# A two-layer decoder trunk on one core: later turns at the feed-forward ends, and attention scores over 128 rows with padded queries

## The chip, the core and the metric

The kernel runs on one core of a Trainium2 chip. The metric is the device time of one launch, in microseconds, as the median of the runs. Engines are named as the profile names them: PE (TensorE, matrix products), PEld (its weight loads), DVE (VectorE), ACT (ScalarE), POOL (GpSimd), SP (SyncE, which issues the weight DMAs).

## The reference

A sequence of 256 tokens of width 2048 goes through two layers, in fp32. Cut to what matters here:

```python
def reference(x, mem, ...):
    for i in range(2):
        if i == 1:
            sk1, sk2, sv = shared_kv(x, kv_norm, w_kv, k_norm, cos, sin)   # 12 heads, keys of 64, values of 128
        u = rms_norm(x, mix_norm[i]) @ w_in[i]
        if i == 0:
            ...                       # causal pooling in four groups
        else:
            q1 = partial_rope(rms_norm(q1, q_norm[b]), cos, sin)    # 12 heads of 64, two maps
            q2 = partial_rope(rms_norm(q2, q_norm[b]), cos, sin)
            o = differential_attention(q1, q2, sk1, sk2, sv, lam)
            token_out = rms_norm(o, subln_norm[b]) * (1.0 - lam_init)
        mem_out = memory_cross_attention(mem_q, mem, ...)           # 4 heads of 128 over 256 memory rows
        x = x + concat(token_out, mem_out) @ w_out[i]
        h = relu(rms_norm(x, ffn_norm[i]) @ w_ff1[i])
        x = x + (h * h) @ w_ff2[i]                                  # width 8192 between
    return x

def differential_attention(q1, q2, k1, k2, v, lam):
    def probs(q, k):
        s = einsum('bqhd,bkhd->bhqk', q, k) * dk ** -0.5
        return softmax(where(key_pos <= q_pos, s, -1e30))
    a = probs(q1, k1) - lam * probs(q2, k2)
    return einsum('bhqk,bkhd->bqhd', a, v)
```

## The kernel before

Activations are held transposed, as tiles of 128 channels by 256 tokens: the residual `resid` is `[128, 16, 256]`. The weights do not fit on the core and are streamed. `Feed.load` brings 128x1024 floats by a DMA from SP, and `Feed._split` turns each block of 512 columns into a rounded half (`hi_ring`, ACT, L147) and the rest (`lo_ring`, DVE, L148), in a ring of six slots, three jobs ahead. Activations are split in the same manner (`split_gain`, ACT L353 and DVE L284; `x_kv` and `x_mx` are two such splits of the residual, with two gains). A product is the sum of high by high, high by low and low by high.

PE goes through the stages in the order of the program: memory keys and values, input projection and pooling of layer 0, its memory heads, `w_out`, the feed-forward part `ffn(0)`; then for layer 1 the shared keys (three `k1` tiles) and values (`v1`), memory keys and values (`mk1`, `mv1`), three `q1` tiles with the differential heads, four memory heads, `w_out`, `ffn(1)` and the output. Steps that are not a product of the stage itself (scores, turns, normalisations) are queued by hand: `at(d, fn)` puts `fn` behind `d` ticks, and `tick()` comes once for four weight blocks. `flush()` runs all that is still queued. So the order on PE is written out; a wait of one queued step holds all PE work behind it.

**The feed-forward part.** `down_tile` (L679 to L706) multiplies one of eight column tiles of the first half of `w_ff2` and gets its bank from `bank()` (tag "st", one buffer); `evict` (L628 to L631) copies the bank to `room` on ACT, and one tick later two DVE adds (L701, L702) put it on `resid` and `done(n)` is called. The second half of the columns is computed from 2x2 block products with fewer multiplications (`slab_jobs`, `product` L711 to L717), summed in seven banks. `last` (L808 to L818) runs the last quarter: the remaining slabs, then `down_tile` for n = 0 to 7; ahead of n = 5 `finish_banks` (L755) combines the seven banks, and queues four `turn(h)` (L773 to L783), at ticks 6 to 9. Each turn is four PE transposes into one bank (`ct`, tag "t", one buffer), one DVE add of 128x512 to `resid` (L781), and `done` for two channel tiles. In layer 0 `done` is `resid_done` (L602): split `x_kv`, then `add_square`, which squares on POOL (L595, the first L589) and adds on POOL (L596) to `acc`. `columns("x")` (from L406) multiplies `acc` by a constant on PE (`tc_x`, L410) for the row norms that scale k1, v1 and q1. In layer 1 `done` is the output DMA.

**The differential heads.** `kT` holds the keys transposed: two heads of 64 lie in the 128 rows of one tile, for each of the two maps. `turn_rows` transposes a pair of heads' queries of both maps in four PE transposes and writes them to `qb` with one ACT copy of 128x512 (L509). `diff_head(h, ...)` queues `scores` (L1113 to L1141), four ticks later `turn` (`dt`, L1146), two ticks after that `pv` (`do`, L1152 to L1154), and three ticks later `back` (`o_t`, L1175). Scores are, for each map, a matmul over the 64 rows of the head, followed by a bf16 matmul of the identity by the mask:

```python
kk = kT[hh : hh + 64, 6 * m + j, :]
nc.tensor.matmul(s1[:, m, :], q[hh : hh + 64, P:T], kk, start=True, stop=False)
nc.tensor.matmul(s1[:, m, P:T], idb, mkb, start=False, stop=True)
```

`s1` is for the second 128 queries against all 256 keys (L1118, L1119), `s0` for the first 128 against 128 keys (L1122, L1123).

Of the kernel before, what the change touches and what calls it, by code (L numbers as in the profile page):

```python
# [10 lines left out]
F32 = mybir.dt.float32  # L11
# [235 lines left out]
def program(ctx, tc, plan, dry, xT, memT, par, lam, cst, wst, yT):  # L247
# [16 lines left out]
    def at(d, fn):  # L264
        pend.setdefault(now[0] + d, []).append(fn)
# [6 lines left out]
    def flush():  # L272
        while pend:
            tick()


    def vt(name):
        return tp.tile([P, T], F32, tag="v", bufs=6, name=name)

    def mmt(name):  # L280
        return pp.tile([P, 512], F32, tag="mm", bufs=3, name=name)
# [42 lines left out]
    def gcol(c):  # L324
        return param[:, c : c + 1]
# [26 lines left out]
    def split_gain(dst, src, g):  # L352
        nc.scalar.activation(dst[:, 0:T], src, AF.Copy, scale=g)  # L353
        stt(dst[:, T : 2 * T], src, g, dst[:, 0:T].bitcast(F32), ALU.mult, ALU.subtract)
# [146 lines left out]
    def turn_rows(raw, i, dst, g):  # L501

        t4 = pp.tile([P, 2, T], F32, tag="t", bufs=1, name="tr")
        for c in range(2):
            for t in range(2):
                nc.tensor.transpose(
                    t4[:, c, t * P : t * P + P], raw[:, t, (i + c) * P : (i + c) * P + P], ident
                )
        nc.scalar.activation(dst, t4, AF.Copy, scale=g)  # L509
# [75 lines left out]
    def add_square(key, src, first, act=False):  # L585

        if first:
            acc[key] = tp.tile([P, T], F32, tag="acc", bufs=1, name="acc")
            nc.gpsimd.tensor_mul(acc[key], src, src)  # L589
            return  # L590
        sq = vt("psq")
        if act:
            nc.scalar.activation(sq, src, AF.Square)
        else:
            nc.gpsimd.tensor_mul(sq, src, src)  # L595
        nc.gpsimd.tensor_add(acc[key], acc[key], sq)  # L596

    def resid_add(ps, n):
        nc.vector.tensor_add(resid[:, n, :], resid[:, n, :], ps[:, 0:T])
        nc.vector.tensor_add(resid[:, n, :], resid[:, n, :], ps[:, T : 2 * T])  # L600

    def resid_done(n, splits):  # L602
        for dst, g in splits:
            split_gain(dst[:, n, :], resid[:, n, :], gcol(g + n))
        add_square("x", resid[:, n, :], n == 0)


    def ffn(l, xs, tags, done):
# [99 lines left out]
        def bank():  # L708
            return pp.tile([P, 512], F32, tag="st", bufs=1, name="x_bank")
# [45 lines left out]
        def finish_banks():  # L755

            p1, p2, p5, p6, p3, p7, p4 = banks
            low = tp.tile([P, 2, 512], F32, tag="rows", bufs=3, name="c_a")
            upp = tp.tile([P, 2, 512], F32, tag="rows", bufs=3, name="c_b")
            c11, c12 = upp[:, 0, :], upp[:, 1, :]  # L760
            u, v = low[:, 0, :], low[:, 1, :]
            add, sub = nc.vector.tensor_add, nc.vector.tensor_sub
            nc.scalar.copy(u, p1)
            nc.scalar.copy(v, p5)
            add(c11, u, p2)
            add(u, u, p6)
            sub(c12, v, u)
            add(u, u, p7)
            add(c12, c12, p3)
            sub(v, v, u)  # L770
            sub(u, u, p4)

            def turn(h):  # L773
                c = 8 + 2 * h
                t4 = pp.tile([P, 2, T], F32, tag="t", bufs=1, name="ct")
                for e in range(2):
                    n = (2 * h + e) // 4
                    w = (2 * h + e) % 4 * P
                    for t, side in enumerate((upp, low)):
                        nc.tensor.transpose(t4[:, e, t * P : t * P + P], side[:, n, w : w + P], ident)  # L780
                nc.vector.tensor_add(resid[:, c : c + 2, :], resid[:, c : c + 2, :], t4)  # L781
                done(c)
                done(c + 1)  # L783

            for h in range(4):
                at(6 + h, lambda h=h: turn(h))

        groups = ((0,), (1, 2), (3,))
        for i in range(NK):
# [18 lines left out]
        def last(q=3):  # L808
            slabs = {0: (0, 1), 1: (2, 3), 2: (4, 5), 3: (6,), 4: (7,)}
            for n in range(8):  # L810
                for i in slabs.get(n, ()):
                    run = slab_jobs(q, i)
                    for j in range(4):
                        run(j)
                        tick()
                if n == 5:
                    finish_banks()
                down_tile(q, n, bank())  # L818

        return last  # L820

# [185 lines left out]
    out_tiles(0, cat, [lead0], [0, 1, 2], fx, last_group)  # L1007

    x_in = []
    down = ffn(0, fx, ("S1", "S0"), lambda n: resid_done(n, [(x_in[0], G_KV)]))  # L1010
    x_kv = sp.tile([P, NK, 512], F32R, tag="S2", name="x_kv")
    x_in.append(x_kv)
    down()
    flush()
    x_mx = sp.tile([P, NK, 512], F32R, tag="S0", name="x_mx")
    for n in range(NK):
        at(10 + 2 * n, lambda n=n: split_gain(x_mx[:, n, :], resid[:, n, :], gcol(G_MIX + 16 + n)))


    kv = sp.tile([P, 6144], F32, tag="big", name="big1")  # L1020
# [25 lines left out]
        return [mmt(name) for _ in range(2)]  # L1046

    c1 = []
    at(6, lambda: c1.extend(columns("x")))
    for c in range(3):  # L1050
        ps = pair_of_banks(c, "k1")
        b_tile(ps, "w_kv", 0, c, x_kv)
# [33 lines left out]
    def carve(n):  # L1086
        off[0] += n
        return att[:, off[0] - n : off[0]]
# [3 lines left out]
    ab = [carve(384) for _ in range(2)]  # L1092
    aTb = [carve(384) for _ in range(2)]
    pT1 = carve(512).rearrange("p (a t) -> p a t", a=2)
    qb = [carve(512).rearrange("p (m t) -> p m t", m=2) for _ in range(4)]
    em1 = [carve(512).rearrange("p (a t) -> p a t", a=2) for _ in range(2)]

    gsub = cp.tile([P, 1], F32, name="gsub")
    nc.vector.tensor_scalar_mul(gsub, gcol(G_SUB), 1.0 - LAM_INIT)
# [4 lines left out]

    cat1 = sp.tile([P, NK, 512], F32R, tag="S1", name="cat1")

    def diff_head(h, q1, q2, y, lag):
        hh = (h % 2) * 64
        j = h // 2
        e1, e0, a, aT = e1b[h % 2], e0b[h % 2], ab[h % 2], aTb[h % 2]  # L1110
        yh = y.rearrange("p (t j m h) -> p t j m h", t=2, j=2, m=2)[:, :, j % 2, :, h % 2]
# [1 line left out]
        def scores():  # L1113
            s1 = pp.tile([P, 2, T], F32, tag="s", bufs=2, name="s1")
            s0 = pp.tile([P, 2, P], F32, tag="s", bufs=2, name="s0")
            for m, q in enumerate((q1, q2)):
                kk = kT[hh : hh + 64, 6 * m + j, :]
                nc.tensor.matmul(s1[:, m, :], q[hh : hh + 64, P:T], kk, start=True, stop=False)  # L1118
                nc.tensor.matmul(s1[:, m, P:T], idb, mkb, start=False, stop=True)  # L1119
            for m, q in enumerate((q1, q2)):  # L1120
                kk = kT[hh : hh + 64, 6 * m + j, 0:P]
                nc.tensor.matmul(s0[:, m, :], q[hh : hh + 64, 0:P], kk, start=True, stop=False)  # L1122
                nc.tensor.matmul(s0[:, m, :], idb, mkb, start=False, stop=True)  # L1123
            mx = tp.tile([P, 4], F32, tag="m4", bufs=6, name="mx")
            z = tp.tile([P, 4], F32, tag="m4", bufs=6, name="z")
            for i, t, s, e in ((0, 1, s1, e1), (2, 0, s0, e0)):
                mi = mx[:, i : i + 2]
                nc.vector.tensor_reduce(out=mi, in_=s, axis=AX.X, op=ALU.max, negate=True)
                nc.vector.tensor_mul(mi, mi, yh[:, t, :])
                for m in range(2):  # L1130
                    nc.scalar.activation(
                        e[:, m, :], s[:, m, :], AF.Exp, bias=mx[:, i + m : i + m + 1],
                        scale=yh[:, t, m : m + 1], accum_out=z[:, i + m : i + m + 1],
                    )
            zr = tp.tile([P, 4], F32, tag="m4", bufs=6, name="zr")
            nc.vector.reciprocal(zr, z)
            zl = tp.tile([P, 2], F32, tag="m2", bufs=12, name="zl")
            nc.vector.tensor_scalar_mul(zl, zr.rearrange("p (i m) -> p i m", m=2)[:, :, 1], nlam)
            for i, e, dst in ((0, e1, a[:, P : P + T]), (1, e0, a[:, 0:P])):
                nc.vector.tensor_scalar_mul(e[:, 1, :], e[:, 1, :], zl[:, i : i + 1])  # L1140
                stt(dst, e[:, 0, :], zr[:, 2 * i : 2 * i + 1], e[:, 1, :], ALU.mult, ALU.add)  # L1141
# [42 lines left out]
    for c in range(3):  # L1184
        ps = pair_of_banks(0, "q1")
        b_tile(ps, "w_in_q", 1, c, x_mx)
        rows, v = query_rows(ps, c1, 64)
        rope(rows, qtab)
        y = query_scale(v, c1)
        for i in range(2):  # L1190
            j = 2 * c + i
            q = qb[j % 4]
            at(4 + i, lambda i=i, q=q, rows=rows: turn_rows(rows, 2 * i, q, qcol))
            for g in range(2):
                diff_head(2 * j + g, q[:, 0, :], q[:, 1, :], y, 6 + (2 if c == 2 else 3) * (2 * i + g))
    for h in range(4):
        ps = mmt("mq1")
        c_tile(ps, "w_in", 1, 12 + h, range(NK), x_mx)
        q, y = mem_query(ps[:, 0:T], mqg1, c1)
        mem_head(  # L1200
            q, y, mk1[:, h, :], lambda mb, h=h: mv1[:, mb, h * P : h * P + P],
            em1[h % 2], pT1, cat1[:, 12 + h, :], 3,
        )

    fx1 = sp.tile([P, NK, 512], F32R, tag="S0", name="fx1")
# [87 lines left out]
```

## Time and profile before

| what | value |
|---|---|
| runs | 2097.9, 2101.76, 2098.39 us |
| median | 2098.39 us |
| profiled execution | 2097.61 us, span 2095.8 us |
| PE clock granted, mean | 0.999 of full speed |
| PE, DVE, ACT, POOL busy | 99%, 83%, 64%, 4% of the span |
| HBM traffic | 185 GB/s over the span |

The span is the stretch between the first and the last instruction of the profiled execution; its own time is 1.8 us longer. A busy share is over the whole span; a stage may look quite different. In a line of grouped instructions stand line, engine and operation, the tiles by name (written <- read), shapes, count, busy time, mean duration of one in ns, and the idle time of the engine ahead of them with what ended it. Matmuls overlap on PE, so the step from one start to the next says what a matmul takes, and the mean duration is longer than that.

### The profile page before, as it was taken

The page shows a single profiled execution, that of the slowest core. Times are in us where ns is not written, and L with a number is a line of the kernel's source. Part 1 is how long each engine was busy: PE and PEld are TensorE (multiplying, and loading weights), DVE is VectorE, ACT ScalarE, POOL GpSimd, SP SyncE. Part 2 cuts the span into 40 slices and gives each one's busy share as a digit, 9 for nine tenths or more (in the row PEclk, how much of TensorE's full clock was granted, in tenths as well). Part 3 has the DMA queues.
Part 4 walks back from the last instruction along what each step waited for, and adds up shares of the span by engine and source line. Part 5 has one row for each costly group of instructions (what it writes and reads, how often), then busy time and mean ns, then how long its engine had stood idle before and what let it go on. Part 6 is the DMA issues. An engine that isn't in the chain of part 4 may idle for free.

```text
span 2095.8 us, 32323 instructions
## 1 busy us (share of the span) xinstructions
PE 2076.5 (99%) x11086; PEld 1755.1 (84%) x11086; DVE 1733.5 (83%) x3210; ACT 1344.4 (64%) x2483; POOL 85.8 (4%) x98
## 2 busy tenths in 40 slices
PE   9999999999999999999999999999999999999998
PEld 7888888888888888777888778888888888888877
DVE  8788888789888878999755687888878878988897
ACT  7765576566667656666655577557656666666664
POOL 0002300000000000014000000310000000000000
PEclk9999999999999999999999999999999999999999
DMA  8555555565555656554565433555556555565554
GB/s 308 171 186 188 181 191 182 186 208 189 192 192 192 209 181 204 177 169 159 190 227 191 141 122 101 194 187 184 188 181 206 191 192 197 185 209 189 192 186 141
DMA packets 110469, 390.75 MB, mean 186 GB/s; under 512 B 12256, under 2 KB 14944, under 8 KB 110304
## 3 DMA queue, kind: packets, MB, share of 16 engines
q1 hardware_dynamic: 110160, 388.59, 55.7%
q8 instruction: 87, 1.43, 0.3%
q14 instruction: 78, 0.64, 0.1%
q10 hardware_dynamic: 144, 0.10, 0.0%
HBM read 386.54 MB, written 2.10 MB: 185 GB/s over the span
## 4 chain that ended last, share of the span: by engine, by line
PE 52%; DVE 2%; ACT 1%; issue 0%; DMA 0%; POOL 0%; DVEq 0%; ACTq 0%
PE x_bank L364 9%; PE x_bank L689 6%; PE x_bank L365 4%; PE wo L364 3%; PE ff L364 3%; PE x_bank L690 3%; PE p L717 2%; PE p L715 2%; PE p L716 2%; PE ff L365 1%; PE wo L365 1%; PE q L388 1%; PE v L390 1%; PE v L388 1%; PE v L389 1%; PE q L390 1%
## 5 line engine op out<-in xcount | busy, mean ns | idle before, releaser
L147 ACT CAST hi_ring<-raw 128x512 fp32r<-128x512 f32 x1193 | 735.6, 620 | 541.5 <-PE x_bank L364 166.1
L148 DVE TENSOR_TENSOR lo_ring<-raw,hi_ring 128x512 fp32r<-128x512 f32 x1193 | 831.7, 704 | 232.9 <-ACT hi_ring L147 215.2
L364 PE MATMUL x_bank<-fx,hi_ring 128*128 128x512 f32 x1536 | 543.8, 397 | 0.0
L365 PE MATMUL x_bank<-fx,lo_ring 128*128 128x256 f32 x1536 | 429.8, 280 | 0.0
L689 PE MATMUL x_bank<-z,hi_ring 128*128 128x512 f32 x1008 | 359.3, 398 | 4.9 <-ACT room L630 3.7
L364 PEld LDWEIGHTS x_bank<-fx,hi_ring 128*128 128x128 f32 x1536 | 288.3, 188 | 75.5 <-ACT room L630 0.8
L365 PEld LDWEIGHTS x_bank<-fx,lo_ring 128*128 128x128 f32 x1536 | 289.6, 189 | 1.4
L690 PE MATMUL x_bank<-z,lo_ring 128*128 128x256 f32 x1008 | 282.7, 281 | 0.2 <-DVE lo_ring L148 0.2
L148 DVE TENSOR_TENSOR lo_ring<-slab,hi_ring 128x1024 fp32r<-128x1024 f32 x192 | 234.8, 1224 | 47.4 <-ACT hi_ring L147 37.6
L147 ACT CAST hi_ring<-slab 128x1024 fp32r<-128x1024 f32 x192 | 200.7, 1047 | 65.6 <-PE p L716 23.6
L689 PEld LDWEIGHTS x_bank<-z,hi_ring 128*128 128x128 f32 x1008 | 189.8, 188 | 55.1 <-ACT room L630 6.1
L690 PEld LDWEIGHTS x_bank<-z,lo_ring 128*128 128x128 f32 x1008 | 190.5, 189 | 3.6 <-DVE lo_ring L148 2.1
L364 PE MATMUL wo<-cat,hi_ring 128*128 128x512 f32 x512 | 182.2, 400 | 0.0
L364 PE MATMUL ff<-fx,hi_ring 128*128 128x512 f32 x512 | 179.9, 397 | 0.0
L365 PE MATMUL wo<-cat,lo_ring 128*128 128x256 f32 x512 | 143.6, 281 | 0.0
L365 PE MATMUL ff<-fx,lo_ring 128*128 128x256 f32 x512 | 142.9, 279 | 0.0
L364 PEld LDWEIGHTS wo<-cat,hi_ring 128*128 128x128 f32 x512 | 96.1, 188 | 23.8 <-DVE cat L284 0.2
L364 PEld LDWEIGHTS ff<-fx,hi_ring 128*128 128x128 f32 x512 | 96.1, 188 | 23.1
L715 PE MATMUL p<-hi_ring,sit 128*128 128x512 f32 x256 | 102.1, 399 | 1.8 <-ACT hi_ring L147 1.5
L717 PE MATMUL p<-lo_ring,sit 128*128 128x512 f32 x256 | 100.5, 396 | 1.1 <-DVE lo_ring L148 1.0
L716 PE MATMUL p<-hi_ring,sit 128*128 128x512 f32 x256 | 100.5, 393 | 0.0
L365 PEld LDWEIGHTS wo<-cat,lo_ring 128*128 128x128 f32 x512 | 96.7, 189 | 0.3
(290 smaller groups left out, 3335.9 us busy)
## 6 DMA issues: line engine op xcount, KB each, us to landing
raw<-in_w SPq DMA_DIRECT2D x595, 512.0 KB, 3.5
slab<-in_w SPq DMA_DIRECT2D x128, 512.0 KB, 3.6
resid<-in_x SPq DMA_DIRECT2D x8, 256.0 KB, 5.4
memraw<-in_mem SPq DMA_DIRECT2D x4, 512.0 KB, 3.6
out_y<-resid SPq DMA_DIRECT2D x16, 128.0 KB, 1.8
memraw<-in_mem SPq DMA_DIRECT2D x7, 256.0 KB, 6.3
raw<-in_w SPq DMA_DIRECT2D x3, 256.0 KB, 3.8
memraw<-in_mem SPq DMA_DIRECT2D x2, 128.0 KB, 4.3
```

What stands on the lines that cost most here:

```text
L147: self.nc.scalar.copy(hi, src)
L148: self.nc.vector.tensor_sub(lo, src, hi.bitcast(F32))
L364: nc.tensor.matmul(ps, hi, xs[:, k, :], start=first and i == 0, stop=False)
L365: nc.tensor.matmul(ps[:, T : 2 * T], lo, xs[:, k, 0:T], start=False, stop=last and i == len(ks) - 1)
L388: nc.tensor.matmul(ps[t], xl, hi, start=k == 0, stop=False)
L389: nc.tensor.matmul(ps[t], xh, hi, start=False, stop=False)
L390: nc.tensor.matmul(ps[t], xh, lo, start=False, stop=k == NK - 1)
L689: nc.tensor.matmul(ps, hi, z[:, i, :], start=a, stop=False)
L690: nc.tensor.matmul(ps[:, T : 2 * T], lo, z[:, i, 0:T], start=False, stop=b)
L715: nc.tensor.matmul(ps, a[1], hi, start=first, stop=False)
L716: nc.tensor.matmul(ps, a[0], hi, start=False, stop=False)
L717: nc.tensor.matmul(ps, a[0], lo, start=False, stop=last)
```

## The change

It has two parts, added together.

**Ends of the feed-forward parts.** The four turns are queued two ticks later (8 to 11). The column tiles n = 6 and 7 of the last quarter get banks of the tag "mm" (three buffers) in place of the one "st" bank. In layer 0 `resid_done` no longer squares; the squares are queued behind `down()`, two for each tick from 2 to 9, on ACT, with their sums on DVE (`later_square`). The `flush()` behind `down()` goes, so turns that are still queued come among the first k1 blocks. The splits of `x_mx` start at tick 14 in place of 10, and `columns("x")` comes at tick 12 in place of 6.

**Scores over 128 rows.** The queries of a pair of heads are written into two tiles, one for each head, whose other 64 rows are zero. The zeros are set once by six DVE memsets for three pairs of tiles, and `turn_queries` writes the 64 rows of each head by an ACT copy of its own. The scores' matmuls then take all 128 rows of `kT` and of the padded tile. `em1`, the exponentials of the memory heads, has one buffer in place of two, which makes room for the tiles.

```diff
@@ -595,14 +595,25 @@
+    def later_square(n):
+
+        if n == 0:
+            acc["x"] = tp.tile([P, T], F32, tag="acc", bufs=1, name="acc")
+            nc.scalar.activation(acc["x"], resid[:, 0, :], AF.Square)
+            return
+        sq = vt("later")
+        nc.scalar.activation(sq, resid[:, n, :], AF.Square)
+        nc.vector.tensor_add(acc["x"], acc["x"], sq)
...
-    def resid_done(n, splits):
+    def resid_done(n, splits, square=True):
         for dst, g in splits:
             split_gain(dst[:, n, :], resid[:, n, :], gcol(g + n))
-        add_square("x", resid[:, n, :], n == 0)
+        if square:
+            add_square("x", resid[:, n, :], n == 0)
@@ -783,7 +794,7 @@
             for h in range(4):
-                at(6 + h, lambda h=h: turn(h))
+                at(8 + h, lambda h=h: turn(h))
@@ -815,7 +826,7 @@
                 if n == 5:
                     finish_banks()
-                down_tile(q, n, bank())
+                down_tile(q, n, bank() if n < 6 else mmt("ff2"))
@@ -1007,14 +1018,15 @@
-    down = ffn(0, fx, ("S1", "S0"), lambda n: resid_done(n, [(x_in[0], G_KV)]))
+    down = ffn(0, fx, ("S1", "S0"), lambda n: resid_done(n, [(x_in[0], G_KV)], False))
     x_kv = sp.tile([P, NK, 512], F32R, tag="S2", name="x_kv")
     x_in.append(x_kv)
     down()
-    flush()
+    for n in range(NK):
+        at(2 + n // 2, lambda n=n: later_square(n))
     x_mx = sp.tile([P, NK, 512], F32R, tag="S0", name="x_mx")
     for n in range(NK):
-        at(10 + 2 * n, lambda n=n: split_gain(x_mx[:, n, :], resid[:, n, :], gcol(G_MIX + 16 + n)))
+        at(14 + 2 * n, lambda n=n: split_gain(x_mx[:, n, :], resid[:, n, :], gcol(G_MIX + 16 + n)))
@@ -1046,7 +1058,7 @@
-    at(6, lambda: c1.extend(columns("x")))
+    at(12, lambda: c1.extend(columns("x")))
@@ -1092,8 +1104,23 @@
-    qb = [carve(512).rearrange("p (m t) -> p m t", m=2) for _ in range(4)]
-    em1 = [carve(512).rearrange("p (a t) -> p a t", a=2) for _ in range(2)]
+    qb = [[carve(512).rearrange("p (m t) -> p m t", m=2) for _ in range(2)] for _ in range(3)]
+    em1 = carve(512).rearrange("p (a t) -> p a t", a=2)
+    for pair in qb:
+        nc.vector.memset(pair[0][64:128], 0.0)
+        nc.vector.memset(pair[1][0:64], 0.0)
+
+    def turn_queries(rows, i, pair):
+        t4 = pp.tile([P, 2, T], F32, tag="t", bufs=1, name="tq")
+        for c in range(2):
+            for t in range(2):
+                nc.tensor.transpose(
+                    t4[:, c, t * P : t * P + P], rows[:, t, (i + c) * P : (i + c) * P + P], ident
+                )
+        for g, r in enumerate((slice(0, 64), slice(64, 128))):
+            nc.scalar.activation(pair[g][r], t4[r], AF.Copy, scale=qcol[r])
@@ -1113,13 +1139,13 @@
-            for m, q in enumerate((q1, q2)):
-                kk = kT[hh : hh + 64, 6 * m + j, :]
-                nc.tensor.matmul(s1[:, m, :], q[hh : hh + 64, P:T], kk, start=True, stop=False)
+            for m in range(2):
+                kk = kT[:, 6 * m + j, :]
+                nc.tensor.matmul(s1[:, m, :], q[:, m, P:T], kk, start=True, stop=False)
                 nc.tensor.matmul(s1[:, m, P:T], idb, mkb, start=False, stop=True)
...
@@ -1189,17 +1215,17 @@
-            q = qb[j % 4]
-            at(4 + i, lambda i=i, q=q, rows=rows: turn_rows(rows, 2 * i, q, qcol))
+            q = qb[j % 3]
+            at(4 + i, lambda i=i, q=q, rows=rows: turn_queries(rows, 2 * i, q))
             for g in range(2):
-                diff_head(2 * j + g, q[:, 0, :], q[:, 1, :], y, 6 + (2 if c == 2 else 3) * (2 * i + g))
+                diff_head(2 * j + g, q[g], y, 6 + (2 if c == 2 else 3) * (2 * i + g))
```

The row blocks of `s0` are changed in the same way, and the memory heads take `em1` in place of `em1[h % 2]`.

More of the change, by code (lines that the diff above doesn't have):

```diff
@@ L1105, in program, with diff_head @@
     cat1 = sp.tile([P, NK, 512], F32R, tag="S1", name="cat1")
-    def diff_head(h, q1, q2, y, lag):
-        hh = (h % 2) * 64
+    def diff_head(h, q, y, lag):
         j = h // 2
@@ L1115, in scores @@
             s0 = pp.tile([P, 2, P], F32, tag="s", bufs=2, name="s0")
-            for m, q in enumerate((q1, q2)):
-                kk = kT[hh : hh + 64, 6 * m + j, :]
-                nc.tensor.matmul(s1[:, m, :], q[hh : hh + 64, P:T], kk, start=True, stop=False)
+            for m in range(2):
+                kk = kT[:, 6 * m + j, :]
+                nc.tensor.matmul(s1[:, m, :], q[:, m, P:T], kk, start=True, stop=False)
                 nc.tensor.matmul(s1[:, m, P:T], idb, mkb, start=False, stop=True)
-            for m, q in enumerate((q1, q2)):
-                kk = kT[hh : hh + 64, 6 * m + j, 0:P]
-                nc.tensor.matmul(s0[:, m, :], q[hh : hh + 64, 0:P], kk, start=True, stop=False)
+            for m in range(2):
+                kk = kT[:, 6 * m + j, 0:P]
+                nc.tensor.matmul(s0[:, m, :], q[:, m, 0:P], kk, start=True, stop=False)
                 nc.tensor.matmul(s0[:, m, :], idb, mkb, start=False, stop=True)
@@ L1201, in program @@
             q, y, mk1[:, h, :], lambda mb, h=h: mv1[:, mb, h * P : h * P + P],
-            em1[h % 2], pT1, cat1[:, 12 + h, :], 3,
+            em1, pT1, cat1[:, 12 + h, :], 3,
         )
```

## The prediction

> **What bounds the kernel now.** I read the page's engine totals first, then the windows of the stages that the diff touches, then the chain, the waits and the grouped lines inside them. Columns of the first fence: busy time, share, instructions.
>
> ```profile
> PE 2076.5 (99%) x11086; PEld 1755.1 (84%) x11086; DVE 1733.5 (83%) x3210; ACT 1344.4 (64%) x2483; POOL 85.8 (4%) x98
> ```
>
> PE is busy 99% of the span, so time can only come out of PE's own work, or out of the few places where PE stands. The windows show the places (start:end, length, then busy time and instructions of PE, PEld, DVE, ACT, POOL, then PE's granted clock, DMA share, GB/s): the layer-0 ends, the attention stage, the end of the kernel.
>
> ```profile
> 940.00:980.00 40.00, 34.57 (x175) 28.51 (x174) 40.00 (x65) 23.12 (x48) 22.24 (x24) 0.96 0.44 144
> 1177.00:1310.00 133.00, 132.68 (x776) 105.92 (x775) 101.47 (x350) 93.68 (x299) 0.00 (x0) 1.00 0.34 108
> 2070.00:2095.80 25.80, 20.50 (x135) 18.02 (x133) 14.05 (x25) 6.92 (x12) 0.00 (x0) 1.00 0.32 112
> ```
>
> At 940 to 980 PE misses 5.4 us while DVE is busy all 40.00 us and POOL 22.24. In the attention stage PE misses 0.3 of 133; only fewer or cheaper matmuls help there, and DVE (76%) and ACT (70%) leave room. At the end PE misses 5.3 us.
>
> **Part 1, scores over 128 rows.** The chain through one head's scores (start, us to the next piece, instruction):
>
> ```profile
> 1200.34 0.63 PE s L1118 x2
> 1200.96 0.16 PE s L1119
> 1201.13 0.63 PE s L1118 x2
> 1201.75 0.16 PE s L1119
> 1201.91 0.41 PE s L1122 x2
> 1202.33 0.16 PE s L1123
> 1202.49 0.42 PE s L1122 x2
> 1202.91 0.16 PE s L1123
> 1203.07 0.22 PE o_t L1175 x2
> ```
>
> One head takes 1203.07 - 1200.34 = 2.73 us. An fp32 matmul is two records ("x2"): 0.63 us with 256 columns, 0.41 with 128, contracting 64 rows. Matmuls with 128 rows and the same columns stand later in the chain:
>
> ```profile
> 1290.23 0.22 PE do L1152 x2
> ...
> 1292.97 0.86 PE mo L571 x4
> ```
>
> `mo` is two matmuls of 256 columns, 0.43 each; `do` is one of 128 columns, 0.22. So each 64-row record costs about 0.1 us more than a 128-row one. Padded with zeros, a head becomes 2 x 0.43 + 2 x 0.22 + the four mask matmuls. No row shows a bf16 mask matmul between 128-row ones. As its ends I take half a 128-column fp32 record (0.06) and today's 0.16, and in between 0.11, the step between 128-column records, because the fp32 weights that follow must load behind it. That gives 0.86 + 0.44 + 0.44 = 1.74, so -0.99 a head and -11.9 for 12 heads (bounds -9.5 and -14.3). A 128-row `ms` L544 behind the short `st_mq` records takes 0.54 for x2; with 0.54 and 0.33 in all four places, a head is 1.08 + 0.66 + 0.44 = 2.18, only -6.6 in all. It stays as the outer bound.
>
> What is added: `turn_queries` has two ACT writes of 64x512 where one of 128x512 stood (L509, 698 ns); six more, each between 0.35 (half the row) and 0.70. Neither shortens PE; ACT has 39 us free in this stage. But the transposes' bank is held up to 0.7 longer, and `do` and `o_t` of heads 1, 2 and 6 arrive with 0.05 to 0.16 us to spare, so I add +0.6 (0 to 2). The six memsets of 64x512 stand on DVE between lo splits in the mk1 stage, where DVE is busy 30 of 50 us; hidden, and at 0.3 to 0.7 each they would cost 4 us at most without that cover. `em1` as one buffer adds no wait, since on PE one head's `mt` turn stands before the next head's scores. Part 1: -11.3.
>
> **Part 2, ends of layer 0.** PE's waits between 935 and 980 (who waited for whom: total, times, longest), and the clock in the stretch behind the longest:
>
> ```profile
> PE ct L780 <- DVE resid L781: 2.6, 1, 2.6
> PE x_bank L689 <- ACT room L630: 1.8, 2, 1.1
> PE tc_x L410 <- POOL acc L596: 1.0, 1, 1.0
> ```
>
> ```profile
> 960.20:963.60 3.40, 3.40 (x13) 3.00 (x13) 3.40 (x6) 2.53 (x7) 3.23 (x5) 0.50 0.43 155
> ```
>
> The turns' transposes wait for DVE to add the turn before (one bank, tag t), and DVE is slow because POOL squares the residual beside it:
>
> ```profile
> L284 DVE SCALAR_TENSOR_TENSOR x_kv<-resid,param,x_kv 128x256 fp32r<-128x256 f32 x5 | 4.4, 904 | 0.0
> L148 DVE TENSOR_TENSOR lo_ring<-raw,hi_ring 128x512 fp32r<-128x512 f32 x3 | 3.0, 993 | 0.0
> ```
>
> The same kinds take 420 and 686 ns at 1980 to 2060, where POOL does nothing. After the idle of 2.7 us PE ran 3.4 us at clock 0.50, which cost about 1.8 us. The Trainium skill, "TensorE: Matmul & The Clock Gate", section "🎯 Why this matters for your kernels", tells one to avoid idle gaps over about 3 us for the clock; by it this gap would not explain the drop and the 1.8 us would stay lost, part 2 being smaller by that. The row shows the drop right behind 2.7 us, so I go by the row.
>
> After the change the order on PE is n=5, n=6, turn 0, 8 matmuls, turn 1, 9, turn 2, 7, turn 3, 8, then k1 without a break. From n=5's start at 942.57 that is 96 matmuls, 48 pairs of 0.23 + 0.12 (chain rows `wo` L364 and L365) = 16.8, and 16 transposes of 0.11 = 1.8: it ends at 961.15. In the trace the same work, with the k1 matmuls between taken out, ends at 967.0. So -5.9 (the sum of 0.90 for n=6's bank, 2.75 for the turn, 1.8 of clock and some 0.4 of small gaps). n=6 goes to the mm bank and no longer waits for the eviction of n=5; between two turns lie 7 to 9 matmuls, 1.2 to 1.6 us, and the add takes 0.67. If DVE's queue holds that add longer, up to 2.7 comes back.
>
> The squares move to ACT (16, at about 0.38 as `mq_sq`) and 15 adds to DVE (0.41), 6.2 us on an engine that is full here. POOL's presence costs DVE 10.7 us in 940 to 978 (each row less its undisturbed duration), so DVE still gets about 4.5 us freer, and `x_mx`'s splits go 4 ticks later. `columns` at tick 12 instead of 6 finds `acc` done some 3 us before: -1.15. With POOL's 8.19 us in 870 to 940 gone, that stretch comes nearer to its twin of layer 1 at 2000 to 2070 (PE busy 67.04 of 70 against 68.52); I take -0.5 (0 to -1.5). Part 2: -7.5 (-5 to -9.5).
>
> **Part 3, end of layer 1.** n=6 and n=7 in the mm banks drop the waits of 0.85 and 0.45 us for the evictions; turns among n=7 end 12 matmuls before its last, so the tail of 3.2 us behind PE changes by 0 to +0.3. -1.3 (-0.8 to -1.6).
>
> **Sum.** -11.3 - 7.5 - 1.3 = -20.1 on the profiled execution's 2097.61 (span 2095.8 and 1.8 around it): 2077.5. The median of the runs, 2098.39, is 0.8 above it: 2078.3. The bounds of the parts give 2073.5 to 2083.5. A measurement of this kernel can tell 0.2%, 4.2 us, from no change.
>
> **Rivals.**
> (a) Rows do not set a matmul's time. Then the 0.1 us per record comes from something else (operands, the switch to bf16), scores gain nothing, and the time is 2078.3 + 11.3 = 2089.6. For it: every 64-row matmul in the trace stands next to a bf16 one. Against it: the gap between the two records of one matmul, with no bf16 between, is 0.32 as well (starts at 1200.27 and 1200.59). Chance 0.08. The Trainium skill, "TensorE: Matmul & The Clock Gate", same section, says that a matmul over 32 rows takes the same time as one over 128, so that padding would buy nothing; the chain rows 0.63 and 0.43 speak against it here.
> (b) DVE and ACT bind in the attention stage. At 1208 to 1216 DVE is busy all 8.0 us, at 1247.4 to 1256 DVE 8.45 and ACT 8.53 of 8.6. If half of the cheaper scores only lets PE reach those stretches earlier, part 1 is -5.7: 2083.9. For it: those two stretches; against it: the stage's means of 76% and 70%. Chance 0.10.
> (c) The turns still wait, since the 15 adds are queued on DVE among the splits. Then 2.75 + 1.8 stay: 2082.9. Chance 0.08.
> (d) Slower. Heads' chains become PE's bound, and the clock follows: when scores end a microsecond earlier, the wait lands on `dt` or `do`. A stop of 2.75 us brings 1.8 us of half clock, 4.6 in all, as at 955.7. Part 1 then turns from -11.3 into a loss; five such heads of 12 cost 23 against 20.1 gained: 2101, and from the fifth on it decides. For it: slack of 0.05 to 0.16 in three heads; against it: `dt` has 1.6 to 6.1 us of slack, and each head has 5 to 7 us of projection beside it. Chance 0.07.
>
> **How the numbers follow.** The forecast as summed has 0.67, with its own range 2073.5 to 2083.5. Reaching to (b) and (c) and the outer bound of the 128-row record, 2073.5 to 2086.0 leaves out (a), (d) and a tail. Faster by over 0.2%: 0.67 + 0.08 + 0.10 + 0.08, less a tail of 0.02 for cases that add up to no change, 0.91; same 0.02; slower 0.07.
>
> **What would show it.** In the after's chain a head's scores should take about 1.7 us, x2 in 256 columns 0.43. Between 940 and 975 no wait of `ct` over 0.5 us, clock 1.00, and DVE's L284 at about 420. At the end, waits of `x_bank` on `room` reduced to one, of 1.2. It is wrong if the score records keep their 0.32, if a wait on DVE of over 2 us stands in 940 to 980, or if PE is below 97% between 1160 and 1300.

## The result, and the profile after

| | before | changed |
|---|---|---|
| median of the runs | 2098.14 us | 2076.62 us |
| runs | 2097.65 to 2101.76 | 2074.88 to 2077.8 |
| profiled execution, span | 2097.61, 2095.8 us | 2074.88, 2073.1 us |

The ratio is 0.9893, 95% interval 0.9876 to 0.991: the changed kernel is 21.5 us faster. Its profile has a span 22.7 us shorter. Engine totals of the changed kernel's page (busy time, share, instructions):

```profile
PE 2061.5 (99%) x11086; PEld 1754.6 (85%) x11086; DVE 1726.8 (83%) x3231; ACT 1352.2 (65%) x2505; POOL 55.6 (3%) x67
```

PE has as many instructions as before and is busy 15.0 us less; the other 7.7 of the 22.7 us are idle time that went. The windows of the changed kernel that stand for the three stages of the prediction (start:end, length, busy PE, PEld, DVE, ACT, POOL, PE's clock, DMA share, GB/s):

```profile
928.00:968.00 40.00, 39.11 (x211) 33.40 (x210) 39.42 (x78) 34.38 (x74) 0.00 (x0) 1.00 0.52 171
1167.00:1289.20 122.20, 121.82 (x780) 105.95 (x779) 100.60 (x351) 97.06 (x305) 0.00 (x0) 1.00 0.36 118
2048.30:2073.00 24.70, 20.22 (x135) 17.98 (x133) 14.12 (x25) 6.87 (x12) 0.00 (x0) 0.97 0.32 111
```

In the first, PE misses 0.9 us of 40 where it missed 5.4, at clock 1.00 in place of 0.96, and POOL does nothing. DVE is still as good as full. In the last, PE misses 4.5 us where it missed 5.3. PE's only wait left from 935 to 985 (who for whom: total, times, longest):

```profile
PE x_bank L700 <- ACT room L641: 0.9, 1, 0.9
```

The waits of the turns (`ct`) and of `columns` (`tc_x`) are gone. In the attention stage PE's own rows show no wait, but two waits are new among those of its weight loads, 0.8 us in all, for ACT to empty the bank of the query transposes (`tq`). The first of them (start, duration, engine, line; idle ahead in brackets):

```profile
1166.17 0.42 PEld L1118 LDWEIGHTS tq<-const,qrow 128*128 128x128 f32 x4 [0.50 <-ACT att L1122]
```

One head's scores in the changed kernel's chain (start, us to the next piece, instruction):

```profile
1187.88 0.43 PE s L1144 x2
1188.32 0.06 PE s L1145
1188.37 0.49 PE s L1144 x2
1188.86 0.06 PE s L1145
1188.92 0.28 PE s L1148 x2
1189.19 0.06 PE s L1149
1189.25 0.28 PE s L1148 x2
1189.53 0.06 PE s L1149
```

A head is 1.71 us in place of 2.73 here. Over all 12 heads, adding the steps from each score or mask record to the next record on PE, the mean is 1.71 against 2.60.

Setting the same PE instruction of both traces side by side gives what each stretch of the program gained, in us. The other columns are experiments told below, each against the same trace of before:

| stretch | changed | scores alone (e1) | ends alone (e2) | POOL squares (e8) | turns at 6 (e9) | st bank (e10) | squares now (e11) | combined (e12) |
|---|---|---|---|---|---|---|---|---|
| slabs of layer 0 | 1.0 | 0.6 | 1.7 | -0.1 | 1.2 | 1.3 | 1.5 | 1.5 |
| from the last slab to the end of k1 | 7.4 | -0.1 | 7.3 | 1.7 | 7.0 | 5.7 | 6.7 | 8.0 |
| q1 to the end of w_out | 11.2 | 11.2 | -1.5 | 11.2 | 11.2 | 11.2 | 11.2 | 12.5 |
| last matmuls, layer 1 | 1.5 | 0.1 | 1.6 | 0.8 | 1.5 | -0.6 | 1.2 | 3.1 |
| tail behind PE | -0.4 | 0.0 | -0.4 | -0.4 | -0.4 | 0.0 | -0.4 | -0.4 |

The first four rows and the tail make 20.7 of the 22.7 for the changed kernel. The other 2.0 lie in stretches that no edit touches (1.4 in w_out of layer 0, 0.8 in the slabs of layer 1, -0.2 in the first 160 us). Such steps of up to 1.7 us stand in the experiments' traces too, in either direction, so stretches are a better measure here than whole spans.

### The profile page after: what moved, and what is told of

It is laid out like the page before. It is cut to its first block, busy times and chain, and to the rows that moved or that the text cites. A ratio compares the mean times of both kernels' runs of the same rounds, so it can differ in the third digit from the quotient of the medians.

```text
span 2073.1 us, 32331 instructions
## 1 busy us (share of the span) xinstructions
PE 2061.5 (99%) x11086; PEld 1754.6 (85%) x11086; DVE 1726.8 (83%) x3231; ACT 1352.2 (65%) x2505; POOL 55.6 (3%) x67
## 4 chain that ended last, share of the span: by engine, by line
PE 53%; ACT 1%; DVE 1%; DMA 0%; issue 0%; DVEq 0%; ACTq 0%
PE x_bank L364 9%; PE x_bank L700 5%; PE x_bank L365 4%; PE wo L364 3%; PE ff L364 3%; PE x_bank L701 3%; PE p L728 2%; PE p L726 2%; PE p L727 2%; PE ff L365 1%; PE wo L365 1%; PE k L388 1%; PE k L390 1%; PE v L388 1%; PE k L389 1%; PE v L390 1%
## 5 line engine op out<-in xcount | busy, mean ns | idle before, releaser
L148 DVE TENSOR_TENSOR lo_ring<-raw,hi_ring 128x512 fp32r<-128x512 f32 x1193 | 827.1, 700 | 223.9 <-ACT hi_ring L147 208.3
L700 PE MATMUL x_bank<-z,hi_ring 128*128 128x512 f32 x960 | 339.9, 396 | 2.1 <-ACT hi_ring L147 1.2
L148 DVE TENSOR_TENSOR lo_ring<-slab,hi_ring 128x1024 fp32r<-128x1024 f32 x192 | 234.3, 1222 | 46.8 <-ACT hi_ring L147 37.5
L701 PE MATMUL x_bank<-z,lo_ring 128*128 128x256 f32 x960 | 268.6, 280 | 0.2 <-DVE lo_ring L148 0.2
L700 PEld LDWEIGHTS x_bank<-z,hi_ring 128*128 128x128 f32 x960 | 180.1, 188 | 48.5 <-ACT hi_ring L147 2.5
L701 PEld LDWEIGHTS x_bank<-z,lo_ring 128*128 128x128 f32 x960 | 181.0, 188 | 3.2 <-DVE lo_ring L148 1.7
```

Source lines behind the costliest of these rows:

```text
L148: self.nc.vector.tensor_sub(lo, src, hi.bitcast(F32))
L700: nc.tensor.matmul(ps, hi, z[:, i, :], start=a, stop=False)
L701: nc.tensor.matmul(ps[:, T : 2 * T], lo, z[:, i, 0:T], start=False, stop=b)
```

## The experiments

**One part alone.** e1 is the kernel before with the hunks on `qb`, `turn_queries`, `scores` and `em1`; e2 is the kernel before with the other hunks.

Each run is compared with the kernel before as measured beside it: 2097.71 us for e1 to e4, 2100.67 for e5 to e8, 2099.23 for e9 to e12.

> The kernel before with the scores part of the change alone. Theory (64-row records cost about 0.1 us more than 128-row ones, and nothing else moves): 11.2 us less than before, ratio 0.9947, with one head's scores at 1.7 us and the span from the first q1 matmul to the last mo some 11 us shorter. Rival (heads' chains become the bound): less than 8 us. Rival (the two parts help each other): this gain and that of the ends alone do not add up to the whole 21.5.

> The kernel before with the ends of the feed-forward parts alone, scores as before. Theory: 8.4 us from the layer-0 end, 1.5 from the layer-1 end, less 0.4 of tail, so 9.5 to 10.5 us less than before, ratio 0.9952. Rival (part of the 22.7 us between the two profiles, 1.4 us in the first 60 us of the span and 0.8 in the slabs of layer 1, belongs to the change): 11 or more.

e1: 2084.49 us against 2097.71, ratio 0.9938 (0.9925 to 0.9952). e2: 2087.61, ratio 0.9954 (0.9941 to 0.9966). By stretch, scores alone bring 11.2 where scores stand and nothing at the ends (the 0.6 in the slabs are of no edit); the ends bring 7.3 and 1.6 where they stand. 13.2 and 10.1 add up to 23.3, with intervals of 3 us on either side of each, so against 21.5 they neither help nor hinder each other visibly. The -1.5 of e2 in the attention stretch is no wait. Its windows (columns as above) show the clock: 0.85 on the mean of 10 us, and 0.50 in the first three of them, with PE busy all the time.

```profile
1250.00:1260.00 10.00, 10.00 (x62) 8.74 (x61) 5.71 (x20) 6.42 (x22) 0.00 (x0) 0.85 0.16 57
1252.00:1253.00 1.00, 1.00 (x7) 1.00 (x7) 1.00 (x5) 0.18 (x1) 0.00 (x0) 0.50 0.00 0
```

**Is it the rows?** e3 is the changed kernel with even heads over 64 rows; e4 is the kernel before without the mask matmuls, so it leaves the causal mask out.

```diff
 e3 (from the changed kernel)
+        r = slice(0, 64) if h % 2 == 0 else slice(0, P)
-                kk = kT[:, 6 * m + j, :]
-                nc.tensor.matmul(s1[:, m, :], q[:, m, P:T], kk, start=True, stop=False)
+                kk = kT[r, 6 * m + j, :]
+                nc.tensor.matmul(s1[:, m, :], q[r, m, P:T], kk, start=True, stop=False)
 e4 (from the kernel before)
-                nc.tensor.matmul(s1[:, m, P:T], idb, mkb, start=False, stop=True)
-                nc.tensor.matmul(s0[:, m, :], idb, mkb, start=False, stop=True)
```

> The changed kernel with even heads contracted over 64 rows again (rows 0 to 63 of the same padded tiles), odd heads over 128. Theory (rows set the price): 6 heads x (2.60 - 1.71) = 5.3 us more than the changed kernel, and within one profile even heads' records stand 0.32 and 0.21 apart, odd heads' 0.215 and 0.11. Rival (the operands or tiles, not the rows): no change.

> The kernel before (64 rows) without the 48 bf16 mask matmuls; the causal mask is left out. Theory (rows set the price): score records stay 0.32 and 0.21 apart, a head takes 4 x 0.32 + 4 x 0.21 = 2.12, so 48 x 0.13 = 6 us less than before, ratio 0.997. Rival (the change between fp32 and bf16 is what costs): records fall to 0.215 and 0.11, a head takes 1.3, 15 us less than before, ratio 0.993.

e3: 2080.43 us, ratio to before 0.9917 (0.9904 to 0.9931). The attention stretch gains 5.5 in place of 11.2, so the six heads cost 5.7: as the theory had it, though the theory that follows below gives the same. e4: 2084.48 us, ratio 0.994 (0.9926 to 0.9953), -13 us, where the theory said -6 and the rival -15. A head takes 1.55 us. The records in its trace tell why, and its chain has the four score records of 256 columns in one piece:

```profile
1174.75 1.06 PE s L1118 x4
```

By their starts the first of the four 64-row matmuls has its two records 0.320 apart, but the ones behind it follow at 0.216, 0.215, 0.216, and those of 128 columns at 0.11, all over 64 rows. A 64-row record that follows a 64-row record costs what a 128-row one does. My theory had fallen, and so had its rival in the form that I gave it. What is left is the change of row count between neighbours.

**Order alone, and the mask over 64 rows.** e5 is the kernel before with a head's four mask matmuls behind its four score matmuls, still over 64 rows and without padding (one start and one stop for each bank). e6 keeps the old order and takes only the head's own 64 rows of the mask, so that bf16 still stands between, but all rows are 64 (only half of the queries are masked). e7 is the changed kernel in e5's order.

```diff
 e5 (from the kernel before)
-                nc.tensor.matmul(s1[:, m, :], q[hh : hh + 64, P:T], kk, start=True, stop=False)
-                nc.tensor.matmul(s1[:, m, P:T], idb, mkb, start=False, stop=True)
+                nc.tensor.matmul(s1[:, m, :], q[hh : hh + 64, P:T], kk, start=m == 0, stop=False)
 ...
+            for s, cols in ((s1, slice(P, T)), (s0, slice(0, P))):
+                for m in range(2):
+                    nc.tensor.matmul(s[:, m, cols], idb, mkb, start=False, stop=m == 1)
 e6 (from the kernel before)
-                nc.tensor.matmul(s1[:, m, P:T], idb, mkb, start=False, stop=True)
+                nc.tensor.matmul(s1[:, m, P:T], idb[hh : hh + 64], mkb[hh : hh + 64], start=False, stop=True)
```

> The kernel before, scores still over 64 rows, with the order alone changed: the four score matmuls of a head first, then its four mask matmuls. New theory (the price is that of a change of row count between neighbours on PE, about 0.1 us for each weight load that can then not be made ahead; a 64-row record itself costs what a 128-row one does): two changes a head in place of eight, a head at 1.31 + 4 x 0.06 + 0.2 = 1.75, some 10 us less than before, ratio 0.995, with no padding. Theory of the prediction (each 64-row record costs 0.1 us more): records stay 0.32 and 0.21 apart, 0 to 3 us less.

> The kernel before with the mask matmuls over the head's own 64 rows, in the old order; this masks only half of the queries. New theory (change of row count): no change of row count is left inside a head, records fall to 0.22 and 0.11 though a bf16 matmul still stands between, a head takes about 1.8, 9 to 10 us less than before, ratio 0.9955. Rival (the change between fp32 and bf16 costs): a head stays at 2.60 and the time at that of before.

> The changed kernel with the masks behind the four score matmuls. If a bf16 neighbour costs the score record behind it some 0.055 us (0.27 where 0.216 is due), three of four such places go: 12 x 3 x 0.055 = 2 us less than the changed kernel, a head at 1.55. If padded rows have taken all there was: no change.

e5: 2087.02 us against 2100.67, ratio 0.9937 (0.9925 to 0.995). e6: 2091.25, ratio 0.9957 (0.9943 to 0.997). e7: 2072.69, ratio 0.9868 (0.9852 to 0.9885). In e5's trace the stretch from q1 to the end of w_out gains 9.7 us. In e7's it gains 13.9, of which 0.9 lies in w_out, which the edit does not touch; up to there it is 13.0, 1.8 more than the changed kernel, about the 2 expected. In e6's it gains 6.2 where 12 x (2.60 - 1.92) is 8.2; the clock was 0.91 from 1250 to 1270, which is 1.8 of it. The chain of e5 through one head:

```profile
1176.21 1.06 PE s L1118 x4
1177.27 0.44 PE s L1121 x4
1177.71 0.33 PE s L1124 x4
```

and of e7, the same order over 128 rows:

```profile
1170.35 0.86 PE s L1144 x4
1171.21 0.44 PE s L1147 x4
1171.65 0.22 PE s L1150 x4
```

The 128-column scores take 0.44 in both. What e5 has more stands at the front of the scores (1.06 against 0.86) and at the front of the masks (0.33 against 0.22), its two changes of row count. The first half of a head in e6:

```profile
1177.88 0.63 PE s L1118 x2
1178.51 0.06 PE s L1119
1178.56 0.49 PE s L1118 x2
```

In e6 the mask takes 0.06 and the score behind it 0.49, as in the changed kernel, though they are 64 rows and a bf16 matmul stands between. So fp32 next to bf16 is not what costs 0.1. What a bf16 mask does cost the score behind it is the 0.06 by which 0.49 is over 0.43; e7 takes three of these places out of each head, hence 1.53 in place of 1.71. All kernels in one table:

| kernel | rows of the scores | mask | changes of row count a head | one head, us |
|---|---|---|---|---|
| before | 64 | between, 128 rows | 8 | 2.60 |
| e6 | 64 | between, 64 rows | 2 | 1.92 |
| e5 | 64 | behind, 128 rows | 2 | 1.77 |
| e4 | 64 | none | 2 | 1.55 |
| changed | 128 | between, 128 rows | 0 | 1.71 |
| e7 | 128 | behind, 128 rows | 0 | 1.53 |

One change costs (2.60 - 1.71) / 8 = 0.11, (1.92 - 1.71) / 2 = 0.11 and (1.77 - 1.53) / 2 = 0.12 us by this count. The count leaves out the record ahead of a head's first score, which takes some 0.09 us more where 64 rows follow. With it the three are 0.12, 0.15 and 0.17. The chain lines of e5 and e7, which hold it, give 0.20 for the change into 64 rows and 0.11 for the change back. The weight loads show where it is paid. First PEld, then PE, in the kernel before (start, duration, engine, line; idle ahead in brackets):

```profile
1200.27 0.29 PEld L1118 LDWEIGHTS s<-big,att 64*128 64x128 f32 x2
1200.89 0.10 PEld L1119 LDWEIGHTS <-idb 128*128 128x128 bf16 x1 [0.33 <-issue]
```

```profile
1200.27 0.70 PE L1118 MATMUL s<-big,att 64*128 64x256 f32 x2
1200.90 0.23 PE L1119 MATMUL s<-mkb,idb 128*128 128x128 bf16 x1
```

The mask's weights are loaded at 1200.89, after an idle of 0.33 that waits for nothing, when the mask matmul itself is due. Of the 24 such loads 23 have this idle time, 7.6 us in all (PEld's waits from 1146 to 1310; in the changed kernel there is none):

```profile
PEld L1119 <- issue: 7.6, 23, 0.3
```

In the changed kernel the same load comes 0.21 us ahead of its matmul, beside the score records:

```profile
1187.94 0.10 PEld L1145 LDWEIGHTS <-idb 128*128 128x128 bf16 x1
```

```profile
1188.15 0.22 PE L1145 MATMUL s<-mkb,idb 128*128 128x128 bf16 x1
```

In e6, where score and mask both have 64 rows, the load is ahead by as much (load at 1178.13, matmul at 1178.35).

The Trainium skill, "TensorEngine Tiling (Array Packing)", section "Key Properties", states that a change of the tiling mode drains the TensorE. The runs fit that if matmuls over 64 and over 128 rows count as two modes, which no trace names. The price of a change here is 0.11 to 0.17 us.

**What made the end of layer 0 faster?** Four edits, each from the changed kernel. e8 squares on POOL as each tile is done; e11 squares at that moment too, but on ACT and DVE; e9 puts the turns at their old ticks. e10 puts n = 6 and 7 back on the one st bank.

```diff
 e8
-    down = ffn(0, fx, ("S1", "S0"), lambda n: resid_done(n, [(x_in[0], G_KV)], False))
+    down = ffn(0, fx, ("S1", "S0"), lambda n: resid_done(n, [(x_in[0], G_KV)]))
-    for n in range(NK):
-        at(2 + n // 2, lambda n=n: later_square(n))
 e9
-                at(8 + h, lambda h=h: turn(h))
+                at(6 + h, lambda h=h: turn(h))
 e10
-                down_tile(q, n, bank() if n < 6 else mmt("ff2"))
+                down_tile(q, n, bank())
 e11
+    def square_now(n):
+        resid_done(n, [(x_in[0], G_KV)], False)
+        later_square(n)
```

> The changed kernel with layer 0's squares and sums on POOL again, as each residual tile is done (no later squares); turns, banks and columns stay late. Theory (POOL slows DVE, whose late lo splits and adds hold PE): the stretch from the last slab of layer 0 to the end of the k1 tiles, 7.4 us shorter in the changed kernel, becomes 2 to 4 us longer again, with L284 beside POOL at 850 to 900 ns. Rival (the later turns and the mm banks alone bring the gain, and DVE has time enough): within 1 us of the changed kernel.

> The changed kernel with the turns two ticks earlier again (6 to 9 in place of 8 to 11), all else kept. Theory (the squares on POOL held DVE, and so the turns; with POOL idle DVE serves the turns in time wherever they stand): within 1 us of the changed kernel. Rival (the prediction's step that the room between the turns counts): turns meet DVE's combining of the seven banks, waits of ct of 2 us or more in either layer, 2 to 5 us more than the changed kernel.

> The changed kernel with the one st bank for n = 6 and 7 too. Theory (the waits for the eviction come back, 0.9 and 0.5 in each layer, and the first matmul of n = 6 can't go ahead of n = 5): 2 to 3 us more than the changed kernel, x_bank waiting for room two times in each layer. Rival (DVE's lo splits would have held PE at those places anyway): under 1 us.

> The changed kernel with the squares on ACT and their sums on DVE, but as each residual tile is done in place of later. If leaving POOL is what counts: within 1 us of the changed kernel. If the lateness counts too (the adds of n = 8 to 15 then stand on DVE between the turns): waits of ct on DVE of 1 us and more, 1 to 4 us more than the changed kernel.

e8: 2082.94 us, ratio 0.9915 (0.9902 to 0.9929). Of the 7.4 us from the last slab to the end of k1 only 1.7 are left, and nothing of the 1.0 in the slabs. PE's waits for the turns in e8 from 925 to 985, and DVE's lines beside POOL (953 to 963):

```profile
PE ct L791 <- DVE resid L792: 3.6, 3, 1.7
```

```profile
L284 DVE SCALAR_TENSOR_TENSOR x_kv<-resid,param,x_kv 128x256 fp32r<-128x256 f32 x5 | 4.0, 853 | 0.0
L148 DVE TENSOR_TENSOR lo_ring<-raw,hi_ring 128x512 fp32r<-128x512 f32 x4 | 3.8, 941 | 0.0
```

Two more waits for DVE stand beside them, 0.7 for `x_kv` and 0.6 for a lo split. The turns wait again, though they stand at their late ticks with 7 to 9 matmuls between them. In the changed kernel the two kinds of DVE's (955 to 968) take 482 ns (L284) and 685 (L148):

```profile
L148 DVE TENSOR_TENSOR lo_ring<-raw,hi_ring 128x512 fp32r<-128x512 f32 x10 | 6.7, 685 | 0.0
L284 DVE SCALAR_TENSOR_TENSOR x_kv<-resid,param,x_kv 128x256 fp32r<-128x256 f32 x8 | 3.4, 482 | 0.0
```

e9: 2074.13 us, ratio 0.9888 (0.9871 to 0.9906), and no wait of a turn in either layer: with POOL idle the old ticks do as well. e11: 2076.57, ratio 0.9888 (0.9871 to 0.9905), no wait of a turn; in its stretch 0.7 us less than the changed kernel gained. That squares come later counts for little. That they left POOL is e8 against e11, with the squares at the same moment in both: 6.7 less 1.7, so 5.0 us of the 7.4. In the slabs it is 1.6, of which little is certain, since e1 differs there by 0.6 without an edit. The later tick of `columns` was not tried by itself; e8, with the sums on POOL and that tick, shows no wait of `tc_x`. e10: 2078.64, ratio 0.9904 (0.989 to 0.9919). The evictions are back, two in each layer, as the theory had it; its stretches lose 1.7 and 2.1 us, somewhat more than the 2 to 3 expected in all. From 2030 to 2076, with one more of 0.2 behind them:

```profile
PE x_bank L700 <- ACT room L641: 2.3, 2, 1.6
```

**A version beyond the change.** e12 groups the masks as e7 does, and combines the seven banks one column tile earlier, where PE's last slab has just filled them:

```diff
-                if n == 5:
+                if n == 4:
                     finish_banks()
-                down_tile(q, n, bank() if n < 6 else mmt("ff2"))
+                down_tile(q, n, bank() if n < 5 else mmt("ff2"))
...
-                at(8 + h, lambda h=h: turn(h))
+                at(12 + h, lambda h=h: turn(h))
```

> A version beyond the change: masks grouped as in the earlier run (0.17 us a head), and the seven banks combined one column tile earlier, behind the last slab (before n = 4), with n = 5, 6 and 7 in the mm banks and the turns at the same place as in the change. If PE's two stops of about 1.1 us before n = 5 (one in each layer, for the eviction of n = 4 and for late lo splits) go: 2 us for them and 2 for the masks, 4 us less than the changed kernel. Rival (DVE is full in the last slabs, so that combining there holds the lo splits): the stops move, and only the 2 us of the masks are left.

2069.18 us, ratio to before 0.9857 (0.9842 to 0.9871): about 7 us under the changed kernel, whose interval it does not touch (it does overlap with e7's). By stretches e12 gains 4.0 us on the changed kernel, as expected: 1.3 from q1 to the end of w_out, 0.6 and 1.6 at the two ends and 0.5 in the slabs. The rest of the 7 lies in stretches without an edit and in the spread of the runs. The two ends gain 8.0 and 3.1 us in place of 7.4 and 1.5. Both stops before n = 5 are gone: PE's only wait at the end of layer 0 is 0.2 us for a turn, and at the end of layer 1 there is none.

## Why the prediction was right, and where its reasons were not

The forecast was 2078.3 us in 2073.5 to 2086.0; the median is 2076.62. The range of the parts, 2073.5 to 2083.5, leaves out the bounds of the +0.6 (0 to 2); added up with them it is 2073.0 to 2085.1.

- **Scores**, forecast -11.3: measured 11.2 in e1 and in the changed kernel, with a head at 1.71 (forecast 1.74), the mask at 0.06 (taken at 0.11) and the score behind a mask at 0.49 and 0.28 (taken at 0.43 and 0.22). The 11.2 are 10.7 in the heads' own records, 1.0 in the records ahead of them and some 0.4 of small differences, less 0.9 lost at the query transposes (next point). The size was right, the reason was not. The step that failed is "each 64-row record costs about 0.1 us more than a 128-row one". In e4 and e5 64-row records stand 0.216 apart; the 0.11 us belongs to a change of row count. The estimate came out because every score matmul of the kernel before stands between two such changes, which is luck: for e5, which moves only the masks, the same step gives 0 to 3 us, and e5 gained 9.7. The argument against rival (a), that the records of one matmul are 0.32 apart with no bf16 between, misread the 0.32: the step from the first record to the second is long only where a 128-row matmul stands ahead of the first (0.320 there in e4, 0.215 in the next matmul). Rival (a) pointed at the right neighbour for the wrong property (bf16, which e6 excludes). The prediction set its rows against the rule of the Trainium skill in rival (a), that few rows take as long as 128; for 64 rows the runs bear the rule out, since 64-row records in a row stand 0.216 apart as 128-row ones do. It does not follow that padding buys nothing.
- **The additions of part 1**, forecast +0.6 (0 to 2): the twelve ACT writes of 64x512 take 684 ns each, nearly what 128x512 took (698), the upper of the two bounds given for them. The bank of the transposes is held that much longer, and the second pair's transposes wait for it in two of the three q1 tiles. The steps ahead of the transposes and between them are 0.9 us longer than before (1.2 in e7). The reason for the term was right, its size a little low.
- **Ends of layer 0**, forecast -7.5: measured 7.4 to the end of k1 and 1.0 in the slabs. For the walk and for `columns` the forecast was 5.9 + 1.15 = 7.05, for the slabs 0.5, which the 0.6 of e1 neither bears out nor refutes. DVE's L284 came at 482 ns, not at 420. The walk gave the turns' wait to POOL and to the new order together; e8, e9 and e11 separate them, and the order has hardly a share. The half clock was put down to the 2.7 us of idle in front of it. That is not shown: the changed kernel has neither, in e8 stops of 1.5 and 1.7 us brought no lower clock (1.00 from 928 to 968), and in e2 the clock was 0.50 with no stop but 0.2 us. So the 1.8 us counted for it may have gone by luck.
- **End of layer 1**, forecast -1.3: 1.5 of matmuls less 0.4 of tail, so 1.1. The one wait left there is not the eviction that was named but a late lo split, 0.9 us, behind DVE's combining of the banks. The tail grew by 0.4, 0.1 over its bound. It did so in every version with n = 6 and 7 in the mm banks and in none without, and the 0.4 stands behind DVE's last add, from whose end to the end of the span it is 3.19 us in place of 2.75; why is open.
- **Rivals.** (b) did not come: nothing of PE's waits in the attention stage but the loads for the query transposes, though DVE went from 76% to 82% busy there and ACT from 70% to 79%. (c) did not come: e11 has the adds among the turns and no turn waits. (d) did not come: no wait of `dt` or `do` stands on PE's rows, and one of 0.2 on PEld's.

The sum of the parts was -20.1; the medians differ by 21.5 and the profiles by 22.7, of which 2.0 lie in untouched stretches.

## What to carry to other kernels

Look at the neighbours of a cheap-looking matmul before costing it by its shape: where matmuls over fewer rows alternate with full ones, put those of one row count together, or pad, whichever is easier; order alone got 9.7 of the 11.2 us here. When an in-order engine that feeds PE is full, look at what slows each of its instructions before moving its work about: taking squares off POOL was worth more than any new tick for the turns. Look for waits on the weight loads as well as on PE: the two that the padding brought stand on PEld alone. Compare stretches between the same two instructions of two traces, since the runs of one kernel can differ by more than such an edit brings (before, beside e9 to e12: 2094.66 to 2103.54).

## What had not been expected of the hardware

A change between 64 and 128 rows on PE costs 0.11 to 0.17 us, and the weight load that follows it is not made ahead (idle 0.33 us "issue" on PEld, against 0.21 us ahead without a change). Row count itself costs nothing: 0.216 us a record of 256 columns with 64 rows or 128. And the clock can fall without a stop: in e2 it was 0.85 from 1250 to 1260 (0.50 to 1253) with PE busy all 10.00 us, at a price of 0.15 x 10 = 1.5 us; the 0.2 us of idle ahead of it stands in the kernel before as well.
